# A hybrid decoder layer: the output projection begins with the first halves of four column tiles, and token sums of squares take fewer fp32 products

## The chip, the cores and the metric

The kernel runs on one core of a Trainium2 chip. The metric is the device time of one execution in microseconds (us). Before the change three runs gave 1185.44, 1186.08 and 1186.83 us; the median is 1186.08 us.

Engines are named as in the profile: PE is TensorE (products), PEld its weight load, DVE is VectorE, ACT is ScalarE, POOL is GpSimd, SP is SyncE, whose queue starts most DMAs. A queue executes its instructions in the order of the program, each when its waits are met.

## The reference

The reference computes one layer of a decoder in float32 for 256 tokens with 2048 channels (`x` below is one token's row):

```
h = rmsnorm(x, g_mix);  proj = h @ w_in            # 2048 x 5200
x = x + concat(pool_mixer(..), dsa_attention(..)) @ w_out      # 2048 x 2048
u = rmsnorm(x, g_ffn) @ w_up                       # 2048 x 11264
x = x + (silu(gate(conv3(u))) * val(conv3(u))) @ w_down        # 5632 x 2048
x = x + (p @ w_ple_proj) * sigmoid(rmsnorm(x, g_ple) @ w_ple_gate)
out = rmsnorm(x, g_final)
# rmsnorm(x, g) = x * (mean(x*x over channels) + 1e-6) ** -0.5 * g
```

The norm of a token is one number, r = (mean of squares + 1e-6)^-0.5. It multiplies a whole row, so the kernel multiplies the products by it afterwards and not their inputs.

## The kernel before, in words

**Layout.** Activations are kept with channels in the 128 partitions and tokens along the free axis: `xt` is [128, 16, 256], 16 tiles of 128 channels by 256 tokens. `hT` holds the layer's input times the gain, split in a rounded part (256 columns) and the rest (256 columns), so that float32 accuracy is had from products of the chip's fp32r kind.

**Units and column tiles.** A weight matrix is read in units of 128 x 1024 floats (`unit`, L74 to L89). The SP queue loads a unit into one of four `raw` buffers, ACT writes the rounded copy `hi` (L87), DVE writes the rest, `lo` = raw - hi (L88), a subtraction that reads two operands in SBUF. `hi` and `lo` of a unit lie in one of three buffers `w`, which the units take in turn, so unit k can be cast only when PE is done with unit k-3. A column tile (128 output channels) of a product with 2048 inputs needs two units, its halves. Each half is eight pairs of products on PE (`cm_matmul`, L143 to L149): `hi` against 512 columns (L147), `lo` against 256 (L148). The sum is built in one of four PSUM buffers of pool `acc` (name `pa`), taken in turn: tile k+4 waits until tile k has been read out.

**Stages.** In order: products with `w_in` and the mixers, the output projection with `w_out` (16 column tiles, L518 to L526), the up stage with `w_up` (88 tiles, two by two: a gate tile and a value tile), the down stage with `w_down` (16 tiles), the per-layer embedding with `w_pg` and the final norm.

**Output projection.** Its 16 input tiles are `catP` (pooling) and `catA` (attention), listed in `cats`. `out_unit(c, ps, h)` does half h of column tile c. Two tiles are taken at a time: both first halves, then both second halves. Among the first halves the last pooling group is mapped (`pool_map`, L470 to L488, its products are L483); the two `catP` tiles that come from it are the last of the second halves. `add_residual` (L179 to L186) adds a tile to `xt`, splits it into `hT` for the next stage and squares each pair of tiles into `ssa`, which holds the running sums of squares, [128, 512]: even tiles' tokens in columns 0 to 255, odd tiles' in 256 to 511.

**Sums of squares of tokens.** `rstd_tok` (L197 to L204) sums `ssa` over its partitions by products with ones: four fp32 products of 128 x 2, one for each half of `ssa` and each 128 tokens, which leave one number for each token in a column, [128, 2]. `rstd_col` and `rstd_of` (L119 to L134) make r from it: DVE scales and adds epsilon (L122), POOL raises to the power -0.5 (L128), DVE does one Newton step (L130, L131, L133). It is called for the mixer's norm (r_mix), the up stage's (r_ffn) and the embedding's (r_ple). Where r is needed along the free axis, `rstd_rows` (L136 to L141) multiplies it by the identity on PE and copies it into `rbc`, [128, 256] (L139, L141).

**Up stage.** `conv` (L542 to L554) takes a finished tile: `cm_evict` (L161 to L165) copies its right half (ACT, L163) into one of three buffers `eb`, adds the left half (DVE, L164), after which the PSUM buffer is free, and multiplies by `rbc` (DVE, L165), after which the `eb` buffer is free. A convolution of three taps over the tokens follows (ACT L549, DVE L551 and L553), then the gate (ACT L558, DVE L559) and a split (L112, L113).

**Order of the work.** The program lists instructions in the order of the functions; a list scheduler then moves them, engine by engine, by its own estimate of when each can start. The order on each engine is fixed before the kernel runs.

Of the kernel before, what the change touches and what calls it, by code (L numbers as in the profile page):

```python
# [10 lines left out]
F32 = mybir.dt.float32  # L11
F32R = mybir.dt.float32r
AF = mybir.ActivationFunctionType
OP = mybir.AluOpType
# [4 lines left out]
P = 128  # L19
S = 256  # L20
D = 2048
KT = D // P
# [4 lines left out]
EPS = 1e-6  # L27
# [10 lines left out]
AT_PG = (112, 1264)  # L38

GAP_G = 88  # L40
GAP_W, GAP_A, GAP_F = 144, 8, 176


C_GMIX, C_GFFN, C_GPLE, C_PS, C_CONV = 0, 16, 32, 48, 56
# [6 lines left out]
def layer(ctx: ExitStack, tc: tile.TileContext, a: dict):  # L51
    nc = tc.nc
    in_order = tc.keep_in_program_order
    V, A, T, G = nc.vector, nc.scalar, nc.tensor, nc.gpsimd
# [9 lines left out]
    rbc = mid[0].tile([P, S], F32, name="rbc")  # L64
    ssa = mid[0].tile([P, 2 * S], F32, name="ssa")
    wraw = ctx.enter_context(tc.tile_pool(name="wraw", bufs=4))
    tmp = ctx.enter_context(tc.tile_pool(name="tmp", bufs=2))
    dram = ctx.enter_context(tc.tile_pool(name="dram", bufs=1, space=DRAM))
    acc = ctx.enter_context(tc.tile_pool(name="acc", bufs=4, space=PSUM))
    aux = ctx.enter_context(tc.tile_pool(name="aux", bufs=4, space=PSUM))  # L70
# [3 lines left out]
    def unit(src, n=1024, keep=None, at=(0, LOW)):  # L74

        nonlocal n_units
        raw = wraw.tile([P, UNIT], F32, name="raw")
        nc.sync.dma_start(raw[:, :n], src)
        if keep:
            hi = keep.tile([P, n], F32R, name="hi", bufs=5)  # L80
            lo = keep.tile([P, n], F32R, name="lo", bufs=5)
        else:
            w = wsp[n_units % 3].tile([P, SLOT], F32R, name="w")
            n_units += 1
            h0, l0 = at if n <= 1024 else (0, UNIT)
            hi, lo = w[:, h0:h0 + n], w[:, l0:l0 + n]
        A.copy(hi, raw[:, :n])  # L87
        V.tensor_sub(lo, raw[:, :n], hi.bitcast(F32))  # L88
        return hi, lo  # L89
# [8 lines left out]
    mhalf = cst.tile([P, 2], F32, name="mhalf")  # L98
    G.memset(mhalf, -0.5)
    ones2 = cst.tile([P, 2], F32, name="ones2")  # L100
# [9 lines left out]
    def split(dst_hi, dst_lo, src, scale=None):  # L110
        if scale is None:
            A.copy(dst_hi, src)  # L112
            V.tensor_sub(dst_lo, src, dst_hi.bitcast(F32))  # L113
        else:
            A.activation(dst_hi, src, AF.Copy, scale=scale)
            V.scalar_tensor_tensor(dst_lo, src, scale, dst_hi.bitcast(F32),
                                   op0=OP.mult, op1=OP.subtract)

    def rstd_col(ssq, name):  # L119
        n = ssq.shape[1]  # L120
        ms = tmp.tile([P, n], F32, name="ms")
        V.tensor_scalar(ms, ssq, 1.0 / D, EPS, op0=OP.mult, op1=OP.add)  # L122
        return rstd_of(ms, name)

    def rstd_of(ms, name):
        n = ms.shape[1]
        r0 = tmp.tile([P, n], F32, name="r0")
        G.tensor_tensor(r0, ms, mhalf[:, :n], op=OP.pow)  # L128
        r1 = tmp.tile([P, n], F32, name="r1")
        V.tensor_mul(r1, r0, r0)  # L130
        V.scalar_tensor_tensor(r1, r1, -0.5, ms, op0=OP.mult, op1=OP.mult)  # L131
        r = cst.tile([P, n], F32, name=name)
        V.scalar_tensor_tensor(r, r1, 1.5, r0, op0=OP.add, op1=OP.mult)  # L133
        return r  # L134

    def rstd_rows(r):  # L136
        ps = aux.tile([P, 512], F32, name="ps")
        for t in range(2):
            T.matmul(ps[:, t * P:(t + 1) * P], r[:, t:t + 1].to_broadcast([P, P]), ident,  # L139
                     start=True, stop=True)  # L140
        V.tensor_copy(rbc, ps[:, :S])  # L141

    def cm_matmul(ps, hi, lo, acts, first, last):  # L143

        for i, act in enumerate(acts):
            w = slice(i * P, (i + 1) * P)
            T.matmul(ps, hi[:, w], act, start=first and i == 0, stop=False)  # L147
            T.matmul(ps[:, :S], lo[:, w], act[:, :S],  # L148
                     start=False, stop=last and i == len(acts) - 1)  # L149

    def tiles(act, kts):
        return [act[:, kt, :] for kt in kts]

    def cm_tile(src, c):
        ps = acc.tile([P, 512], F32, name="pa")
        for h in range(2):
            hi, lo = unit(src[c][:, h * 1024:(h + 1) * 1024])
            cm_matmul(ps, hi, lo, tiles(hT, range(8 * h, 8 * h + 8)), h == 0, h == 1)
        return ps

    def cm_evict(dst, ps):  # L161
        b = mid[1].tile([P, S], F32, name="eb", bufs=3)
        A.copy(b, ps[:, S:])  # L163
        V.tensor_add(b, ps[:, :S], b)  # L164
        V.tensor_mul(dst, b, rbc)  # L165
# [13 lines left out]
    def add_residual(c, ps, gcol):  # L179

        xs = xt[:, c, :]
        V.tensor_add(xs, ps[:, :S], xs)
        V.tensor_add(xs, ps[:, S:], xs)
        split(hT[:, c, :S], hT[:, c, S:], xs, prm[:, gcol + c:gcol + c + 1])
        if c % 2:
            square(c // 2)  # L186

    def square(i):
        pair = xt[:, 2 * i:2 * i + 2, :].rearrange("p k s -> p (k s)")
        if i == 0:  # L190
            A.activation(ssa, pair, AF.Square)
        else:
            sq = tmp.tile([P, 2 * S], F32, name="sq", bufs=1)
            A.activation(sq, pair, AF.Square)
            V.tensor_add(ssa, ssa, sq)

    def rstd_tok(name):  # L197

        ps = aux.tile([P, 512], F32, name="ps")
        for t in range(2):  # L200
            for h in range(2):
                T.matmul(ps[:, 2 * t:2 * t + 2], ssa[:, h * S + t * P:h * S + (t + 1) * P], ones2,
                         start=h == 0, stop=h == 1)
        return rstd_col(ps[:, 0:4:2], name)  # L204


    with ExitStack() as c1:
# [117 lines left out]
        for j in range(IH // 2):  # L325
            ps = cm_tile(a["w_qi"], j) if j else ps_q
# [187 lines left out]
        def out_unit(c, ps, h):  # L514
            hi, lo = unit(a["w_out"][c][:, h * 1024:(h + 1) * 1024])
            cm_matmul(ps, hi, lo, cats[8 * h:8 * h + 8], h == 0, h == 1)

        for c0 in range(0, KT, 2):  # L518
            ps2 = [acc.tile([P, 512], F32, name="pa") for _ in range(2)]
            for h in range(2):  # L520
                for e in range(2):
                    out_unit(c0 + e, ps2[e], h)
                    if c0 + h + e == 0:
                        pool_map(*done.pop())
            for e in range(2):
                add_residual(c0 + e, ps2[e], C_GFFN)  # L526


    pin = ctx.enter_context(tc.tile_pool(name="pin", bufs=1))
# [4 lines left out]
    with ExitStack() as c2:  # L534
        far = c2.enter_context(tc.tile_pool(name="far", bufs=1))
        far.tile([P, GAP_F], F32, name="gap_f")
        aT = far.tile([P, NF, 2 * S], F32R, name="aT")
        r_ffn = rstd_tok("r_ffn")
        rstd_rows(r_ffn)
        nu = 0  # L540

        def conv(ps, c):  # L542
            nonlocal nu
            u = ub[:, nu % NU, :]
            nu += 1
            cm_evict(u[:, 2:], ps)
            k = 4 * c
            t = far.tile([P, S], F32, name="cv", bufs=4)
            A.activation(t, u[:, 2:], AF.Identity, bias=cnv[:, k + 3:k + 4],  # L549
                         scale=cnv[:, k + 2:k + 3])  # L550
            V.scalar_tensor_tensor(t, u[:, 1:S + 1], cnv[:, k + 1:k + 2], t,  # L551
                                   op0=OP.mult, op1=OP.add)
            V.scalar_tensor_tensor(t, u[:, :S], cnv[:, k:k + 1], t, op0=OP.mult, op1=OP.add)  # L553
            return t  # L554

        def up_pair(c, ps2):
            ts = [conv(ps2[e], 2 * c + e) for e in range(2)]
            A.activation(ts[0], ts[0], AF.Silu)  # L558
            V.tensor_mul(ts[0], ts[0], ts[1])  # L559
            split(aT[:, c, :S], aT[:, c, S:], ts[0])  # L560

        ps2 = [acc.tile([P, 512], F32, name="pa") for _ in range(2)]
        for h in range(2):
            for e in range(2):
                hi, lo = unit(a["w_up"][e][:, h * 1024:(h + 1) * 1024])
                cm_matmul(ps2[e], hi, lo, tiles(hT, range(8 * h, 8 * h + 8)), h == 0, h == 1)
        up_pair(0, ps2)
        for c in range(1, NF):  # L570
            up_pair(c, [cm_tile(a["w_up"], 2 * c + e) for e in range(2)])


        for c in range(KT):
            ps = acc.tile([P, 512], F32, name="pa")
            for k0 in range(0, NF, 8):
                k1 = min(k0 + 8, NF)
                hi, lo = unit(a["w_down"][c][:, k0 * P:k1 * P], (k1 - k0) * P)
                cm_matmul(ps, hi, lo, tiles(aT, range(k0, k1)), k0 == 0, k1 == NF)
            add_residual(c, ps, C_GPLE)  # L580
# [175 lines left out]
```

## Time and profile before

| | |
|---|---|
| median of three runs | 1186.08 us |
| the profiled execution | 1187.71 us |
| its span, first to last instruction | 1185.9 us |
| PE busy | 1172.4 us, 99% |
| DVE busy | 854.6 us, 72% |
| ACT busy | 643.7 us, 54% |
| POOL busy | 9.0 us, 1% |
| chain that ended last | PE 98% |
| output projection begins, up stage begins | 260.2 us, 352.6 us |
| last product of the down stage begins | 1072.2 us |

The profile's busy time of PE is modelled, and its matmuls are pipelined; what a product costs is better read from the starts of the products around it. A row of the timeline gives start, duration, engine, line, operation, output <- inputs and shapes; several like instructions are merged into one row ("x8"), whose duration runs from the first start to the last end. An fp32 product leaves two records. A group row ends with busy time and mean duration in ns, and after the bar the idle time before the instructions with what ended it.

### The profile page before, as it was taken

The numbers are of one execution on the slowest core, as the hardware profiler recorded it, in microseconds if no ns is written. First come the engines' busy times: TensorE is split into PE (matmuls) and PEld (weight loads), VectorE is DVE, ScalarE is ACT, GpSimd is POOL, SyncE is SP. The second block draws the span as 40 slices with busy tenths as digits, with TensorE's granted clock in tenths as the row PEclk, the third lists the DMA queues.
The fourth block names the chain that finished last, engine by engine and source line by source line (L and its number), as shares of the span: only waits on it lengthen the run. The fifth ranks groups of instructions, "written<-read, shape, count | busy, mean of one in ns | idle before, by whom it ended". The sixth has DMA issues, their size and how long they took to land.

```text
span 1185.9 us, 17860 instructions
## 1 busy us (share of the span) xinstructions
PE 1172.4 (99%) x6804; PEld 1037.6 (87%) x6804; DVE 854.6 (72%) x1308; ACT 643.7 (54%) x943; POOL 9.0 (1%) x27
## 2 busy tenths in 40 slices
PE   9999999999999999999999999999999999999996
PEld 8988888888888888888888888888888888888886
DVE  6578977976678888888888888888555555554564
ACT  7466444554546666666666666666444444444563
POOL 0000000000000000000000000000000000000000
PEclk9999999999999999999999999999999999999998
DMA  8656765545565556556555556556666666666662
GB/s 310 212 175 190 236 215 173 162 147 189 189 194 185 195 194 195 195 192 194 192 194 193 195 192 195 192 196 194 186 194 194 195 194 191 191 193 226 191 214 75
DMA packets 66933, 229.09 MB, mean 193 GB/s; under 512 B 7872, under 2 KB 9672, under 8 KB 66720
## 3 DMA queue, kind: packets, MB, share of 16 engines
q1 hardware_dynamic: 63696, 221.91, 58.5%
q10 hardware_dynamic: 2144, 3.41, 0.9%
q0 software_dynamic: 1008, 2.64, 0.7%
q8 instruction: 53, 0.87, 0.3%
q14 instruction: 32, 0.26, 0.1%
HBM read 224.77 MB, written 3.68 MB: 193 GB/s over the span
## 4 chain that ended last, share of the span: by engine, by line
PE 98%; DMA 0%; ACT 0%; DVE 0%; SPq 0%; issue 0%; POOLq 0%; ACTq 0%
PE pa L147 55%; PE pa L148 28%; PE pa L175 3%; PE pa L176 3%; PE pa L174 3%; PE ps L176 1%; PE ps L175 1%; PE ps L174 1%; DMA raw<-in_w_first 0%; PE ps L483 0%; PE ps L393 0%; PE ps L147 0%; PE ps L310 0%; PE ps L311 0%; PE ps L607 0%; PE ps L444 0%
## 5 line engine op out<-in xcount | busy, mean ns | idle before, releaser
L88 DVE TENSOR_TENSOR w<-raw,w 128x1024 fp32r<-128x1024 f32 (+3 forms) x420 | 503.2, 1199 | 220.8 <-ACT w L87 214.0
L147 PE MATMUL pa<-hT,w 128*128 128x512 f32 x1904 | 652.5, 391 | 0.0
L87 ACT CAST w<-raw 128x1024 fp32r<-128x1024 f32 (+3 forms) x420 | 433.0, 1031 | 341.6 <-PE pa L148 250.6
L148 PE MATMUL pa<-hT,w 128*128 128x256 f32 x1904 | 529.6, 278 | 0.0
L147 PEld LDWEIGHTS pa<-hT,w 128*128 128x128 f32 x1904 | 357.5, 188 | 75.0 <-issue 0.6
L148 PEld LDWEIGHTS pa<-hT,w 128*128 128x128 f32 x1904 | 358.5, 188 | 0.3
L147 PE MATMUL pa<-aT,w 128*128 128x512 f32 x704 | 239.4, 390 | 0.0
L148 PE MATMUL pa<-aT,w 128*128 128x256 f32 x704 | 194.6, 276 | 0.0
L147 PEld LDWEIGHTS pa<-aT,w 128*128 128x128 f32 x704 | 132.2, 188 | 27.5
L148 PEld LDWEIGHTS pa<-aT,w 128*128 128x128 f32 x704 | 132.3, 188 | 0.0
L163 ACT COPY eb<-pa 128x256 f32<-128x256 f32 x119 | 44.2, 372 | 138.7 <-PE pa L148 138.5
L164 DVE TENSOR_TENSOR eb<-pa,eb 128x256 f32<-128x256 f32 x119 | 50.3, 423 | 59.8 <-ACT eb L163 59.6
L175 PE MATMUL pa<-w,hT 128*128 128x512 f32 (+2 forms) x178 | 64.8, 364 | 0.1
L176 PE MATMUL pa<-w,hT 128*128 128x512 f32 (+2 forms) x178 | 64.5, 363 | 0.0
L174 PE MATMUL pa<-w,hT 128*128 128x512 f32 (+2 forms) x178 | 58.0, 365 | 1.3 <-ACT w L87 1.3
L549 ACT ACTIVATE cv<-ub,cnv 128x256 f32<-128x256 f32 x88 | 52.9, 602 | 0.5 <-DVE ub L165 0.2
L147 PE MATMUL pa<-catA,w 128*128 128x512 f32 x128 | 46.9, 396 | 0.8 <-ACT w L87 0.8
L147 PE MATMUL pa<-catP,w 128*128 128x512 f32 x128 | 47.0, 396 | 0.0
L553 DVE SCALAR_TENSOR_TENSOR cv<-ub,cnv,cv 128x256 f32<-128x256 f32 x88 | 42.6, 485 | 3.0
L551 DVE SCALAR_TENSOR_TENSOR cv<-ub,cnv,cv 128x256 f32<-128x256 f32 x88 | 42.0, 479 | 0.1
L165 DVE TENSOR_TENSOR ub<-eb,rbc 128x256 f32<-128x256 f32 x88 | 37.3, 425 | 3.0
L174 PEld LDWEIGHTS pa<-w,hT 128*128 128x128 f32 x178 | 32.8, 188 | 5.8 <-ACT w L87 2.0
(171 smaller groups left out, 848.1 us busy)
## 6 DMA issues: line engine op xcount, KB each, us to landing
raw<-in_w_up SPq DMA_DIRECT2D x176, 512.0 KB, 4.6
raw<-in_w_down SPq DMA_DIRECT2D x80, 512.0 KB, 3.9
raw<-in_w_qk SPq DMA_DIRECT2D x32, 512.0 KB, 4.2
raw<-in_w_out SPq DMA_DIRECT2D x32, 512.0 KB, 4.5
raw<-in_w_pg SPq DMA_DIRECT2D x32, 512.0 KB, 4.0
raw<-in_w_first SPq DMA_DIRECT2D x15, 552.0 KB, 5.8
raw<-in_w_qi SPq DMA_DIRECT2D x16, 512.0 KB, 4.0
raw<-in_w_u SPq DMA_DIRECT2D x16, 512.0 KB, 3.9
```

What stands on the lines that cost most here:

```text
L87: A.copy(hi, raw[:, :n])
L88: V.tensor_sub(lo, raw[:, :n], hi.bitcast(F32))
L147: T.matmul(ps, hi[:, w], act, start=first and i == 0, stop=False)
L148: T.matmul(ps[:, :S], lo[:, w], act[:, :S], start=False, stop=last and i == len(acts) - 1)
L163: A.copy(b, ps[:, S:])
L164: V.tensor_add(b, ps[:, :S], b)
L174: T.matmul(pss[t][:, :n], xh, hi[:, w], start=first and i == 0, stop=False)
L175: T.matmul(pss[t][:, :n], xh, lo[:, w], start=False, stop=False)
L176: T.matmul(pss[t][:, :n], xl, hi[:, w], start=False, stop=last and i == len(kts) - 1)
L549: A.activation(t, u[:, 2:], AF.Identity, bias=cnv[:, k + 3:k + 4], scale=cnv[:, k + 2:k + 3])
L551: V.scalar_tensor_tensor(t, u[:, 1:S + 1], cnv[:, k + 1:k + 2], t, op0=OP.mult, op1=OP.add)
L553: V.scalar_tensor_tensor(t, u[:, :S], cnv[:, k:k + 1], t, op0=OP.mult, op1=OP.add)
```

## The change

There are three edits.

1. In the output projection the first four column tiles are taken together: four first halves, then four second halves. The other twelve tiles go two by two as before. The number of products, units and bytes is the same.
2. `rstd_tok` first adds the two halves of `ssa` on DVE (128 x 256) and then needs two products instead of four. It remains in use for r_mix and r_ple.
3. For the up stage a new function, `rstd_all`, replaces `rstd_tok` and `rstd_rows`. One fp32 product of a matrix of ones with `ssa` (256 columns) puts every token's sum into every partition, so r is computed at once as a row in all partitions: the scaling (L213 of the new file), the power on POOL (L214), the Newton step (L215 to L217), each on 128 x 256 instead of 128 x 2. Its result is `rbc` itself. The scratch tile is `sq` of pool `tmp`.

A spacer, `GAP_W`, grows by 8 columns (32 bytes a partition), while the small tile `r_ffn` is gone.

```
-GAP_W, GAP_A, GAP_F = 144, 8, 176
+GAP_W, GAP_A, GAP_F = 152, 8, 176
...
     def rstd_tok(name):
 
         ps = aux.tile([P, 512], F32, name="ps")
+        V.tensor_add(ssa[:, :S], ssa[:, :S], ssa[:, S:])
         for t in range(2):
-            for h in range(2):
-                T.matmul(ps[:, 2 * t:2 * t + 2], ssa[:, h * S + t * P:h * S + (t + 1) * P], ones2,
-                         start=h == 0, stop=h == 1)
+            T.matmul(ps[:, 2 * t:2 * t + 2], ssa[:, t * P:(t + 1) * P], ones2,
+                     start=True, stop=True)
         return rstd_col(ps[:, 0:4:2], name)
+
+    def rstd_all():
+
+        ps = aux.tile([P, 512], F32, name="ps")
+        V.tensor_add(ssa[:, :S], ssa[:, :S], ssa[:, S:])
+        T.matmul(ps[:, :S], ones2[:, :1].to_broadcast([P, P]), ssa[:, :S], start=True, stop=True)
+        two = tmp.tile([P, 2 * S], F32, name="sq", bufs=1)
+        ms, r0 = two[:, :S], two[:, S:]
+        V.tensor_scalar(ms, ps[:, :S], 1.0 / D, EPS, op0=OP.mult, op1=OP.add)
+        G.tensor_tensor(r0, ms, mhalf[:, :1].to_broadcast([P, S]), op=OP.pow)
+        V.tensor_mul(rbc, r0, r0)
+        V.scalar_tensor_tensor(rbc, rbc, -0.5, ms, op0=OP.mult, op1=OP.mult)
+        V.scalar_tensor_tensor(rbc, rbc, 1.5, r0, op0=OP.add, op1=OP.mult)
...
-        for c0 in range(0, KT, 2):
-            ps2 = [acc.tile([P, 512], F32, name="pa") for _ in range(2)]
+        for c0, cn in ((0, 4), *((c, 2) for c in range(4, KT, 2))):
+            pss = [acc.tile([P, 512], F32, name="pa") for _ in range(cn)]
             for h in range(2):
-                for e in range(2):
-                    out_unit(c0 + e, ps2[e], h)
+                for e in range(cn):
+                    out_unit(c0 + e, pss[e], h)
                     if c0 + h + e == 0:
                         pool_map(*done.pop())
-            for e in range(2):
-                add_residual(c0 + e, ps2[e], C_GFFN)
+            for e in range(cn):
+                add_residual(c0 + e, pss[e], C_GFFN)
...
-        r_ffn = rstd_tok("r_ffn")
-        rstd_rows(r_ffn)
+        rstd_all()
```

Three places show how instructions are moved. A name with a number is one buffer or one use of it: `w_3939` is a unit's hi/lo pair, `pa_3661` a tile's sum, `eb_3712` its copy. Lines from 200 on are those of the new file in the rows of the changed kernel.

The first place is DVE at the beginning of the up stage. Before, the chain of r_ffn (L122 to L133), the copy into `rbc` (L141) and the first multiplication by it (L165) stand among the first subtractions:

```order
L122 TENSOR_SCALAR ms_3509<-ps_3504 128x2
L130 TENSOR_TENSOR r1_3513<-r0_3511 128x2
L164 TENSOR_TENSOR eb_3608<-pa_3522,eb_3608 128x256
L131 SCALAR_TENSOR_TENSOR r1_3513<-r1_3513,ms_3509 128x2
L133 SCALAR_TENSOR_TENSOR r_ffn_3516<-r1_3513,r0_3511 128x2
L88 TENSOR_TENSOR w_3652<-raw_3650,w_3652 128x1024
L164 TENSOR_TENSOR eb_3616<-pa_3523,eb_3616 128x256
L88 TENSOR_TENSOR w_3674<-raw_3672,w_3674 128x1024
L141 COPY rbc_77<-ps_3518 128x256
L165 TENSOR_TENSOR ub_106<-eb_3608,rbc_77 128x256
```

Now, on the same engine at the same place (`w_3664` is the first unit of the fourth tile, `w_3939` the first of the ninth, tiles counted from 1):

```order
L88 TENSOR_TENSOR w_3642<-raw_3640,w_3642 128x1024
L213 TENSOR_SCALAR sq_3506<-ps_3503 128x256
L164 TENSOR_TENSOR eb_3606<-pa_3513,eb_3606 128x256
L88 TENSOR_TENSOR w_3664<-raw_3662,w_3664 128x1024
...
L88 TENSOR_TENSOR w_3939<-raw_3937,w_3939 128x1024
L215 TENSOR_TENSOR rbc_77<-sq_3506 128x256
L216 SCALAR_TENSOR_TENSOR rbc_77<-rbc_77,sq_3506 128x256
L217 SCALAR_TENSOR_TENSOR rbc_77<-rbc_77,sq_3506 128x256
L165 TENSOR_TENSOR ub_106<-eb_3598,rbc_77 128x256
L165 TENSOR_TENSOR ub_106<-eb_3606,rbc_77 128x256
L165 TENSOR_TENSOR ub_106<-eb_3704,rbc_77 128x256
```

Between the scaling (L213) and the Newton step (L215) stand eleven subtractions L88, from `w_3664` to `w_3939`, and the multiplications L165 of the first three tiles are behind them. The power on POOL lies between L213 and L215.

The second place is ACT a little later, in the changed kernel. `cv_3602` is the first tile's convolution, and `eb_3712` the copy of the fourth tile, whose PSUM buffer the eighth tile takes:

```order
L87 CAST w_3876<-raw_3874 128x1024
L87 CAST w_3897<-raw_3895 128x1024
L87 CAST w_3939<-raw_3937 128x1024
L562 ACTIVATE cv_3602<-ub_106,cnv_96 128x256
L163 COPY eb_3712<-pa_3661 128x256
```

The copy of the fourth tile stands behind the cast of the ninth tile's first unit and behind the first tile's convolution; before, each tile's copy stood among the casts of the next tile.

The third place is PE in the output projection, at the step from the third unit of `w_out` to what follows. Before, both second halves (`w_2762`, `w_2783`) belong to the two tiles just begun (`pa_2692`, `pa_2693`), and their last products use the two late `catP` tiles; a third tile (`pa_2811`) begins between them. One row is given for each step to another unit:

```order
L147 MATMUL pa_2692<-catA_2080,w_2762 128x512
...
L147 MATMUL pa_2811<-catP_117,w_2815 128x512
...
L147 MATMUL pa_2693<-catA_2080,w_2783 128x512
L147 MATMUL pa_2692<-catP_117,w_2762 128x512
...
L147 MATMUL pa_2812<-catP_117,w_2836 128x512
L147 MATMUL pa_2811<-catA_2080,w_2857 128x512
```

Now the first halves of the third and fourth tile (`w_2763`, `w_2784`) come in between:

```order
L147 MATMUL pa_2693<-catP_117,w_2763 128x512
...
L147 MATMUL pa_2691<-catA_2079,w_2805 128x512
...
L147 MATMUL pa_2694<-catP_117,w_2784 128x512
L147 MATMUL pa_2691<-catP_117,w_2805 128x512
...
L147 MATMUL pa_2692<-catA_2079,w_2826 128x512
```

Behind the third and fourth tile's first halves the second halves of tiles one and two (`w_2805`, `w_2826`) follow, and no new tile begins among them.

## Rows read from the trace of the kernel before

**Rows 1.** The page: busy time by engine; the chain that ended last.
```profile
PE 1172.4 (99%) x6804; PEld 1037.6 (87%) x6804; DVE 854.6 (72%) x1308; ACT 643.7 (54%) x943; POOL 9.0 (1%) x27
...
PE 98%; DMA 0%; ACT 0%; DVE 0%; SPq 0%; issue 0%; POOLq 0%; ACTq 0%
```

**Rows 2.** Timeline of PE: start us, us, engine, line, names, shapes; sums for r_ffn.
```profile
360.55 0.95 PE L202 MATMUL ps<-ones,ssa 128*128 128x2 f32 x8
...
361.56 0.40 PE L147 MATMUL pa<-hT,w 128*128 128x512 f32 x1
```

**Rows 3.** Timeline of PE: one fp32 product of 256 columns among pairs.
```profile
181.50 0.59 PE L393 MATMUL ps<-qk 128*128 128x256 f32 x2
...
182.04 0.40 PE L147 MATMUL pa<-hT,w 128*128 128x512 f32 x1
```

**Rows 4.** Timeline of PE: r_ffn turned into rows.
```profile
366.56 0.61 PE L139 MATMUL ps<-ident,r_ffn 128*128 128x128 f32 x4
...
367.13 0.40 PE L147 MATMUL pa<-hT,w 128*128 128x512 f32 x1
```

**Rows 5.** Timeline of PE in the output projection, from 275.5 us.
```profile
275.51 0.28 PE L148 MATMUL pa<-catP,w 128*128 128x256 f32 x1
...
277.10 0.50 PE L147 MATMUL pa<-catA,w 128*128 128x512 f32 x1 [0.84 <-ACT w L87]
...
277.66 0.39 PE L147 MATMUL pa<-catP,w 128*128 128x512 f32 x1
...
278.01 0.39 PE L147 MATMUL pa<-catP,w 128*128 128x512 f32 x1
```

**Rows 6.** Timeline of POOL: four of the five powers.
```profile
59.33 1.77 POOL L128 TENSOR_TENSOR r<-ms,mhalf 128x2 f32<-128x2 f32 x1 [57.92 <-DVE ms L122]
...
361.78 0.73 POOL L128 TENSOR_TENSOR r<-ms,mhalf 128x2 f32<-128x2 f32 x1 [128.46 <-DVE ms L122]
1083.39 0.69 POOL L128 TENSOR_TENSOR r<-ms,mhalf 128x2 f32<-128x2 f32 x1 [720.88 <-DVE ms L122]
1168.04 0.55 POOL L128 TENSOR_TENSOR r<-ms,mhalf 128x1 f32<-128x1 f32 x1 [83.96 <-DVE ms L624]
```

**Rows 7.** Timeline of DVE: a subtraction at 59.31, and one at 363.47.
```profile
59.31 1.23 DVE L88 TENSOR_TENSOR w<-raw,w 128x1024 fp32r<-128x1024 f32 x1
...
363.47 1.23 DVE L88 TENSOR_TENSOR w<-raw,w 128x1024 fp32r<-128x1024 f32 x1 [0.17 <-ACT w L87]
```

**Rows 8.** Timeline of PE: tiles four and eight of the up stage begin.
```profile
370.56 0.39 PE L147 MATMUL pa<-hT,w 128*128 128x512 f32 x1
...
392.32 0.39 PE L147 MATMUL pa<-hT,w 128*128 128x512 f32 x1
```

**Rows 9.** Groups of DVE and ACT, 390 to 867 us, by form.
```profile
L88 DVE TENSOR_TENSOR w<-raw,w 128x1024 fp32r<-128x1024 f32 x175 | 214.1, 1224 | 32.2 <-ACT w L87 26.9
...
L551 DVE SCALAR_TENSOR_TENSOR cv<-ub,cnv,cv 128x256 f32<-128x256 f32 x83 | 39.7, 479 | 0.0
L165 DVE TENSOR_TENSOR ub<-eb,rbc 128x256 f32<-128x256 f32 x82 | 34.9, 425 | 2.8
...
L87 ACT CAST w<-raw 128x1024 fp32r<-128x1024 f32 x175 | 184.1, 1052 | 83.7 <-PE pa L148 82.4 <-issue 1.3
L549 ACT ACTIVATE cv<-ub,cnv 128x256 f32<-128x256 f32 x82 | 49.4, 602 | 0.2
L163 ACT COPY eb<-pa 128x256 f32<-128x256 f32 x82 | 30.5, 372 | 96.5 <-PE pa L148 96.5
```

**Rows 10.** Engines by stretch: length, busy PE, PEld, DVE, ACT, POOL; clock, DMA.
```profile
390.60:867.00 476.40, 476.40 (x2805) 421.70 (x2804) 386.42 (x594) 286.40 (x426) 0.00 (x0) 1.00 0.60 193
...
1176.00:1178.40 2.40, 0.00 (x0) 0.00 (x0) 1.49 (x4) 0.91 (x3) 0.09 (x1) 1.00 0.00 0
1178.40:1185.90 7.50, 0.00 (x0) 0.00 (x0) 1.36 (x5) 1.33 (x2) 0.46 (x1) 0.50 0.42 140
```

**Rows 11.** Timeline of PE: its first products.
```profile
1.17 3.48 PE L226 MATMUL ps<-rbc 128*128 128x256 f32 x8 [1.17 <-POOL rbc L104]
```

## The prediction

> **What bounds the kernel.** I read the page first. PE is busy for 99% of the span and makes up 98% of the chain that ended last [rows 1], so a microsecond that PE works less or waits less is a microsecond of the result, and so is one that it waits more. Next comes PE's timeline, for the products that the change removes and for PE's waits. The reader should go by the starts there: one pair of L147 and L148 takes 0.35 us in the output projection (277.66 to 278.01) [rows 5] and 0.34 us in the up stage (64 pairs from 370.56 to 392.32) [rows 8]. Last come POOL's powers [rows 6] and what DVE did beside them [rows 7], because the change puts a power of 256 columns where one of 2 was. POOL is busy 1% of the time [rows 1], but that says nothing of an instruction that does not occur yet.
>
> **The gains.** A stretch of the timeline costs its length less the L148 that lies in it, a third of a pair (its share of the columns), 0.12 us. Eight records of L202 took 361.56 - 360.55 - 0.12 = 0.89 us [rows 2]. For r_mix and r_ple half of them go: 2 x 0.445 = 0.89 us. For the up stage all eight go, and the four records of L139, 367.13 - 366.56 - 0.12 = 0.45 us [rows 4]; a product of 256 columns comes, which by its like costs 182.04 - 181.50 - 0.12 = 0.42 us [rows 3]. That is 0.92 us, all before the fourth tile of the up stage.
>
> In the output projection PE lost time from 275.51 to 277.66: 2.15 us for two pairs, so 1.45 us of waiting, on a cast (L87) [rows 5]. The unit that it waited for needed the buffer of a second half, whose last products use the late `catP` tiles. In the new order two more first halves lie ahead of these, 5.6 us of PE's work. I take the whole 1.45 us as gained; the other end is nothing, or a new wait of that size.
>
> Gains together: 0.89 + 0.92 + 1.45 = 3.3 us. The added DVE sums (three of 128 x 256, 0.43 us each by L165 [rows 9]) stand before subtractions that DVE does well ahead of the product which reads them; were that cover gone, they cost 0.43 us each. The spacer and the vanished small tile cost nothing by themselves; should addresses matter to PE, the price is that of the pace rival below.
>
> **The power.** One column took 0.55 us, two columns 0.69 and 0.73 us where nothing lay beside them [rows 6], so the second column cost 0.14 to 0.18 us. No row shows more than two. If each column costs that, 256 columns take 0.55 + 255 x 0.14 = 36.3 us, or 46.5 us by 0.18. The other end is that columns beyond the first are nearly free, about 1 us. I take 36.3 us, since only these rows show the operation, and the smaller step was the later one.
>
> It starts after the scaling L213, which DVE does behind the sixth unit's subtraction. That one ended at 363.47 + 1.23 = 364.70 [rows 7] and comes 0.89 us earlier, at 363.8; with 0.42 for L213 the power starts at about 364.3 and ends at 400.6.
>
> **The first wait: DVE held.** The power at 59.33 took 1.77 us in place of 0.69 or 0.73 [rows 6]. It is the only one with a subtraction L88 beside it, from 59.31 to 60.54 [rows 7], and it ended 0.56 us after that, which is a power's own time. So the power did not run beside an instruction that reads two operands in SBUF. I choose to read this as exclusion both ways: whoever starts first holds the other off to its end. The price of the other reading, a first call that is slow for its own sake, is the first rival.
>
> [...]
>
> Then the subtraction of `w_3664`, the fourth tile's first unit, waits until 400.6, and everything behind it in DVE's queue with it. It takes 1.22 us [rows 9], to 401.85 with the hand-over. PE has the first three tiles' units by then and begins the fourth at 370.56 - 0.92 = 369.64 [rows 8]; its first product needs only `hi`, its second needs `lo`, at 369.87. PE waits 32.0 us (no exclusion: 0; a step of 0.18: 42.2).
>
> **The second wait: the order behind the power.** L215 to L217 stand in DVE's queue behind the subtraction of `w_3939`. That unit's cast needs the buffer of the seventh tile's second unit, so it begins when PE is done with the seventh tile, and by then all four PSUM buffers are full: `rbc` does not exist, three tiles sit in `eb`, and the eighth tile needs the fourth's buffer. From the end of the seventh tile to the first product of the eighth there follow, by [rows 9], the cast 1.05, the subtraction 1.22, L215 0.43, L216 and L217 0.48 each, the first L165 0.43, the first tile's convolution on ACT (it stands ahead of the copy) 0.60, the copy 0.37 and L164 0.42: 5.5 us, and 0.2 for hand-overs, 5.7 us. This comes whatever the power costs.
>
> **What follows from the waits.** DVE has 476.4 - 386.4 = 90 us to spare in 476.4 [rows 10], 19%. At the second restart it owes the convolutions of seven tiles, and about 19 instructions of some 0.43 us and one subtraction stand ahead of the first `lo` that PE lacks: 9.4 us, where three finished units give PE 8.2 us of work. So 1.2 us are lost there and something at the next units; I take 2.0 us, between 0 and 5.
>
> [...] The first eight records of the program took 3.48 us, 0.43 each [rows 11], against 0.21 for the same form later [rows 3]: a cold start loses about 1.6 us before the rate doubles. I take it to fall in both waits: 3.2 us, between 0 and 3.4.
>
> **The sum.** -3.3 + 32.0 + 5.7 + 2.0 + 3.2 = +39.6 us. The profiled execution took 1187.71 us, 1.8 us of it outside its span of 1185.9, and would take 1227.3 us. It was 1.6 us above the median of the runs, 1186.08 us, against which the result will be read: 1225.7 us. With the bounds of the parts, mostly the step of 0.18, this case reaches from 1219 to 1240 us.
>
> **Rivals.**
> No exclusion, but a long power. DVE goes on with its subtractions, and L215 waits for 400.6 instead of for `w_3939`. Then 0.43 + 0.48 + 0.48 + 0.43 + 0.60 + 0.37 + 0.42 + 0.2 = 3.4 us bring PE to 404.0, where the eighth tile would have begun at 392.32 - 0.92 = 391.4: 12.6 us, with 2.0 and one cold start 1.6, less 3.3: +12.9 us, 1199.0 us. For it: the trace shows only POOL held up, and the 1.77 us belong to the first call. Against: the end 0.56 us behind the subtraction's end. Chance 18%.
>
> A short power. The step from one to two columns is then a start-up step, and the power ends after about a microsecond. The first wait vanishes, the second stays: -3.3 + 5.7 + 2.0 + 1.6 = +6.0 us, 1192.1 us. Against it: two powers of two columns agree within 0.04 us, and both are longer than the one of one column. Chance 15%. [...]
>
> A slower pace afterwards. PE ran at 0.35 us a pair before r_ffn's products and at 0.34 behind them [rows 5, 8]. If PE comes out of the waits at 0.35, the 81 tiles from the eighth on (16 pairs each) and the down stage (16 tiles of 44 pairs) make 2000 pairs: +20 us on the forecast, 1245.7 us. For it: the pace has no cause in the program that I can see. Against: nothing but that it held for 700 us. Chance 18%.
>
> Faster. The power is short and PE does not wait at the eighth tile, so that only the gains remain: 1182.8 us. The place is the copy of the fourth tile; it decides when the chain of 5.7 us from the seventh tile's end falls under 3.3 us. Against it stands that each link is there in the order of DVE or ACT and has a measured length. Chance 4%.
>
> **How the numbers follow.** The forecast has 40%, and 5% are left for a power that costs still more per column than 0.18 us. The range 1197 to 1250 us takes in the forecast, the slower pace and the long power without exclusion; the short power and the faster case, 19%, are mostly left out. A difference under 0.2%, 2.4 us, can't be told from none. Faster has 3%, no difference 3% (the rest of the last rival and the best of the short power), slower 94%.
>
> **What would show it.** The power L214 in POOL's rows: 36 us (right), about 1 us (the short power). A subtraction L88 that begins only when it ends, and PE waiting for DVE in the fourth tile for 32 us, show the exclusion; subtractions that go on beside it show the first rival. PE waiting some 6 us before the eighth tile shows the second wait. In the output projection no product should wait for a cast. A pair's length behind 440 us tells the pace. The forecast is wrong if POOL's row is short or DVE is not held.

## The result and the profile after

The changed kernel is slower: 1.0115 times the kernel before (95% interval 1.0102 to 1.0129) in the first comparison, and 1.0132 (1.0116 to 1.0147) in a second one with more runs, 1201.18 us against 1185.47. That is +13.6 to +15.7 us, where the forecast had +39.6. The sign held and the size did not; the time lies at the first rival's 1199.0 us. Three of the first six runs, and some later ones of kernels with this wait, took 1220 to 1228 us at the same granted clock of 0.99 and stand outside the comparisons; why they differ is open. The rows of this section are from an execution of 1200.92 us.

The page of the profile after, with busy time by engine and the chain that ended last, answers to [rows 1]:

```profile
PE 1171.0 (98%) x6786; PEld 1037.3 (87%) x6786; DVE 855.2 (71%) x1310; ACT 643.8 (54%) x943; POOL 48.4 (4%) x27
...
PE 95%; POOL 3%; DVE 1%; ACT 0%; DMA 0%; issue 0%; SPq 0%; POOLq 0%; ACTq 0%
```

POOL's busy time grew from 9.0 to 48.4 us, and POOL now has 3% of the chain that sets the end. PE's busy time fell by 1.4 us while the span grew by 13.2, so what grew is the time in which PE does nothing. The list of PE's waits (tile and line that waited, on whom: total us, times, longest) has three rows:

```profile
PE pa L147 <- DVE eb L164: 16.5, 1, 16.5
PE ps L239 <- POOL rbc L104: 1.2, 1, 1.2
PE pa L174 <- ACT w L87: 0.4, 1, 0.4
```

The second of these was there before [rows 11]. The first is the loss, and POOL's timeline has its source. It answers to [rows 6]:

```profile
57.99 0.70 POOL L128 TENSOR_TENSOR r<-ms,mhalf 128x2 f32<-128x2 f32 x1 [56.59 <-DVE ms L122]
358.98 41.17 POOL L214 TENSOR_TENSOR sq<-sq,mhalf 128x256 f32<-128x256 f32 x1 [127.22 <-DVE sq L213]
```

The power lasts 41.17 us, to 400.15. The groups of DVE from 358.9 to 400.2 us, by form, show what ran beside it (busy us, mean ns, then the idle time before them and who ended it); compare [rows 7]:

```profile
L88 DVE TENSOR_TENSOR w<-raw,w 128x1024 fp32r<-128x1024 f32 x11 | 13.5, 1225 | 14.7 <-ACT w L87 14.7
L164 DVE TENSOR_TENSOR eb<-pa,eb 128x256 f32<-128x256 f32 x2 | 0.8, 425 | 1.6 <-ACT eb L163 1.6
L215 DVE TENSOR_TENSOR rbc<-sq 128x256 f32<-128x256 f32 x1 | 0.4, 426 | 10.8 <-POOL sq L214 10.8
```

Eleven subtractions ran inside the power, each in 1225 ns, which is what they take with POOL idle [rows 9]. DVE was not held. Its idle time beside the power was spent on casts (14.7 us) and copies (1.6 us), and at the end it stood 10.8 us for the power's result. The last of the eleven, that of `w_3939`, and L215 behind it:

```profile
388.19 1.23 DVE L88 TENSOR_TENSOR w<-raw,w 128x1024 fp32r<-128x1024 f32 x1 [1.57 <-ACT w L87]
400.19 0.43 DVE L215 TENSOR_TENSOR rbc<-sq 128x256 f32<-128x256 f32 x1 [10.77 <-POOL sq L214]
```

PE's timeline at the eighth tile answers to the second row of [rows 8]:

```profile
386.80 0.28 PE L148 MATMUL pa<-hT,w 128*128 128x256 f32 x1
403.62 0.77 PE L147 MATMUL pa<-hT,w 128*128 128x512 f32 x1 [16.55 <-DVE eb L164]
...
404.40 0.63 PE L147 MATMUL pa<-hT,w 128*128 128x512 f32 x1
...
405.04 0.63 PE L147 MATMUL pa<-hT,w 128*128 128x512 f32 x1
...
408.24 0.45 PE L147 MATMUL pa<-hT,w 128*128 128x512 f32 x1
...
408.64 0.39 PE L147 MATMUL pa<-hT,w 128*128 128x512 f32 x1
```

The first seven tiles are multiplied by 387.1; the eighth has no PSUM buffer until the fourth is copied out, and that copy needs a free `eb`, which needs `rbc`. The first product starts 403.62 - 400.15 = 3.5 us behind the power's end. Then seven pairs take 0.64 us each. The windows (length, busy PE, PEld, DVE, ACT, POOL, granted clock, DMA share, GB/s) say why:

```profile
387.00:391.00 4.00, 0.07 (x1) 0.00 (x0) 1.23 (x1) 1.04 (x1) 4.00 (x1) 1.00 0.52 175
391.60:403.60 12.00, 0.00 (x0) 0.01 (x1) 3.31 (x9) 1.58 (x5) 8.55 (x1) 0.50 0.06 20
403.60:408.20 4.60, 4.58 (x14) 3.93 (x15) 4.34 (x13) 3.66 (x8) 0.00 (x0) 0.50 0.00 0
408.20:412.00 3.80, 3.80 (x24) 3.36 (x23) 3.76 (x9) 3.77 (x9) 0.00 (x0) 0.98 0.00 0
```

PE had no products from 387.1; the granted clock was 1.00 up to 391.0 and 0.50 from 391.6, and rose 4.6 us after the restart. In that time 403.62 to 408.24 hold seven pairs that take 7 x 0.34 = 2.4 us elsewhere: 2.2 us lost. Behind 408.6 PE has no further wait in the up stage.

In the output projection the wait of [rows 5] is gone: the list of PE's waits above has no L147 that waited for a cast. Around the same place a pair takes its 0.35 us (274.97 to 275.32):

```profile
274.97 0.39 PE L147 MATMUL pa<-catP,w 128*128 128x512 f32 x1
275.20 0.28 PE L148 MATMUL pa<-catP,w 128*128 128x256 f32 x1
275.32 0.40 PE L147 MATMUL pa<-catA,w 128*128 128x512 f32 x1
```

### The profile page after: what moved, and what is told of

Same layout as the page of the kernel before. It is cut to its first block, busy times and chain, and to the rows that moved or that the text cites. A ratio compares the mean times of both kernels' runs of the same rounds, so it can differ in the third digit from the quotient of the medians.

```text
span 1226.3 us, 17826 instructions
## 1 busy us (share of the span) xinstructions
PE 1197.8 (98%) x6786; PEld 1049.6 (86%) x6786; DVE 858.4 (70%) x1310; ACT 643.2 (52%) x943; POOL 48.4 (4%) x27
## 4 chain that ended last, share of the span: by engine, by line
PE 94%; POOL 3%; DVE 1%; DMA 0%; ACT 0%; SPq 0%; issue 0%; POOLq 0%; ACTq 0%
PE pa L147 53%; PE pa L148 27%; POOL sq L214 3%; PE pa L175 3%; PE pa L176 3%; PE pa L174 3%; PE ps L175 1%; PE ps L176 1%; PE ps L174 1%; DMA raw<-in_w_first 0%; PE ps L496 0%; PE ps L406 0%; PE ps L147 0%; PE ps L323 0%; PE ps L324 0%; PE ps L620 0%
## 5 line engine op out<-in xcount | busy, mean ns | idle before, releaser
L147 PE MATMUL pa<-hT,w 128*128 128x512 f32 x1904 | 672.3, 396 | 16.5 <-DVE eb L164 16.5
L88 DVE TENSOR_TENSOR w<-raw,w 128x1024 fp32r<-128x1024 f32 (+3 forms) x420 | 503.4, 1199 | 242.2 <-ACT w L87 236.1
L148 PE MATMUL pa<-hT,w 128*128 128x256 f32 x1904 | 536.0, 282 | 0.0
L147 PEld LDWEIGHTS pa<-hT,w 128*128 128x128 f32 x1904 | 358.0, 188 | 101.4 <-issue 17.5
L148 PEld LDWEIGHTS pa<-hT,w 128*128 128x128 f32 x1904 | 359.1, 189 | 0.4
L147 PE MATMUL pa<-aT,w 128*128 128x512 f32 x704 | 248.8, 396 | 0.0
L148 PE MATMUL pa<-aT,w 128*128 128x256 f32 x704 | 197.7, 281 | 0.0
L147 PEld LDWEIGHTS pa<-aT,w 128*128 128x128 f32 x704 | 132.0, 188 | 32.4
L148 PEld LDWEIGHTS pa<-aT,w 128*128 128x128 f32 x704 | 132.2, 188 | 0.0
L164 DVE TENSOR_TENSOR eb<-pa,eb 128x256 f32<-128x256 f32 x119 | 50.3, 423 | 68.7 <-ACT eb L163 68.5
L214 POOL TENSOR_TENSOR sq<-sq,mhalf 128x256 f32<-128x256 f32 x1 | 41.2, 41172 | 127.2 <-DVE sq L213 127.2
L147 PE MATMUL pa<-catP,w 128*128 128x512 f32 x128 | 45.9, 391 | 0.0
L147 PE MATMUL pa<-catA,w 128*128 128x512 f32 x128 | 45.6, 390 | 0.0
L165 DVE TENSOR_TENSOR ub<-eb,rbc 128x256 f32<-128x256 f32 x88 | 37.2, 424 | 2.8
```

The lines of the kernel that those rows point to most:

```text
L148: T.matmul(ps[:, :S], lo[:, w], act[:, :S], start=False, stop=last and i == len(acts) - 1)
L214: G.tensor_tensor(r0, ms, mhalf[:, :1].to_broadcast([P, S]), op=OP.pow)
```

## The experiments

Two theories stood at the start. A: the power's length is the price, through the order of the eighth tile, as in the first rival; DVE is not held. B: the power costs something by itself, or the rest of the change is slow too. Each kernel ran beside the kernel before on the same chip.

**The change again, nothing edited** (a_again).

> The changed kernel once more, for a trace of it whose pairs run at 0.34 us. Long power without exclusion (the first rival, now the leading theory): about 1200.6 us, POOL's power about 41 us, subtractions on DVE of 1.23 us beside it, one wait of PE of about 17 us before the eighth tile of the up stage and none in the fourth. Exclusion (the forecast's mechanism): a wait of some 32 us in the fourth tile. Pace theory (the pairs' length is the cost and the wait is not): where pairs take 0.34 us throughout, the time is that of the kernel before.

Measured: 1201.18 us, ratio 1.0132 (1.0116 to 1.0147). The rows above are from it: one wait of 16.5 us before the eighth tile and none in the fourth, although the pairs behind the wait take 0.340 us.

**All but the rows** (b_columns): the new projection order and the sums by fewer products stay, the up stage gets its r by columns.

```
-GAP_W, GAP_A, GAP_F = 152, 8, 176
+GAP_W, GAP_A, GAP_F = 144, 8, 176
...
-        rstd_all()
+        r_ffn = rstd_tok("r_ffn")
+        rstd_rows(r_ffn)
```

> The change with r_ffn made by columns as before (two products, power of 2 columns, turned into rows); first halves of four tiles and two products for each sum stay. Long power: nothing of the cost is left, and the gains show: 0.45 us for each of three sums and 1.45 us in the output projection, 2.8 us, and up to 2.6 us more if the output projection keeps the faster pace of pairs: 1181 to 1184 us, ratio 0.996 to 0.998. If the output projection's new order were the cause (its end leaves PE or the buffers in a worse state): 1198 to 1201 us.

Measured: 1181.67 us, ratio 0.9968 (0.9956 to 0.9979). It beats both kernels. So everything that the change loses is in the rows. Its trace also tells whether DVE holds POOL up; the rows of DVE and of POOL:

```profile
357.51 1.23 DVE L88 TENSOR_TENSOR w<-raw,w 128x1024 fp32r<-128x1024 f32 x1
```

```profile
357.68 1.65 POOL L128 TENSOR_TENSOR r<-ms,mhalf 128x2 f32<-128x2 f32 x1 [125.91 <-DVE ms L122]
```

A power of two columns that comes 0.17 us behind a subtraction ends 0.59 us after that ends; at 59.33 in the kernel before it was 0.56 us [rows 6, 7]. It is not the first power of this kernel: that one, at 57.98 with no subtraction running, took 0.70 us. So the 1.77 us of the kernel before were a hold-up of POOL by DVE, and not a slow first call. The other traces agree: every power of two columns that began while an L88 ran took 1.65 to 1.77 us (five powers in five kernels), every other 0.69 to 0.73 us, also where an L88 began while the power ran.

**The rows alone** (c_rows_only): the kernel before with `rstd_all` for the up stage; projection and the other sums as before. The function itself is added as in the change.

```
-GAP_W, GAP_A, GAP_F = 144, 8, 176
+GAP_W, GAP_A, GAP_F = 152, 8, 176
...
-        r_ffn = rstd_tok("r_ffn")
-        rstd_rows(r_ffn)
+        rstd_all()
```

> The kernel before with r_ffn alone made as rows at once; output projection in pairs and four products for the other sums as before. Long power: the whole wait of 16 to 17 us and 1.7 us of cold clock, less 0.9 us of products: 1186 + 17 = 1203 us, ratio about 1.014. If the output projection's order were the cause: 1185 us.

Measured: 1229.26 us, ratio 1.0366 (1.0336 to 1.0397): missed by some 26 us. The power takes 41.17 us again and PE waits 16.5 us at the eighth tile again, so the miss lies elsewhere. The count of L147 in 200 us of the up stage shows it (stretch, length, busy PE with the count, clock, DMA share, GB/s); first this kernel, then the changed one:

```profile
440.00:640.00 200.00, 200.00 (x568) 1.00 0.57 187
```

```profile
440.00:640.00 200.00, 200.00 (x589) 1.00 0.59 194
```

With no wait in that stretch and the clock at 1.00 in both, a pair takes 200 / 568 = 0.352 us instead of 200 / 589 = 0.340. Over the 2000 pairs behind the wait this is 25 us. The pace of the prediction's third rival exists, and something sets it. With the old order of the projection the pairs took 0.35 us ahead of the product too (115 L147 from 300 to 340 us).

**No power** (d_no_power): the changed kernel, with a multiplication in the power's place; the up-stage norm is left out.

```
-        G.tensor_tensor(r0, ms, mhalf[:, :1].to_broadcast([P, S]), op=OP.pow)
+        G.tensor_tensor(r0, ms, mhalf[:, :1].to_broadcast([P, S]), op=OP.mult)
```

> The changed kernel with a multiplication on POOL in place of the power (the up stage's norm is then left out and the output is another). All else of the rows is there: the product of 256 columns, the scaling, the Newton step on 128 x 256. Long power: no wait is left, 1181 to 1184 us. If the rows cost by their product, their 128 x 256 instructions on DVE or their place in the order: still 6 us or more above the kernel before, 1192 us.

Measured: 1201.97 us, ratio 1.0139 (1.0124 to 1.0155): missed by 18 us or more, and by chance near the changed kernel's time. POOL's instruction takes 0.62 us, PE has no wait in the up stage and the mean granted clock is 0.997, as in the kernel before, so all that theory A prices is gone. What came instead is the pace:

```profile
440.00:640.00 200.00, 200.00 (x572) 1.00 0.57 188
```

It is 0.350 us behind the 256-column product (356.80), and 0.347 from 800 to 860 us (173 L147); before that product it was 0.340. In the changed kernel too the pairs take 0.35 us from the product on, until PE stops; behind the stop, with the clock back at 1.00, they take 0.340.

The edit changes the order as well: the scheduler has put L215 ahead of the next subtraction, where the changed kernel has eleven between. So the wait's end is not due to the shorter instruction alone.

```profile
359.92 0.41 DVE L215 TENSOR_TENSOR rbc<-sq 128x256 f32<-128x256 f32 x1
```

**Half the power** (h_half): the power on 128 columns, a multiplication on the rest.

```
-        G.tensor_tensor(r0, ms, mhalf[:, :1].to_broadcast([P, S]), op=OP.pow)
+        G.tensor_tensor(r0[:, :P], ms[:, :P], mhalf[:, :1].to_broadcast([P, P]), op=OP.pow)
+        G.tensor_tensor(r0[:, P:], ms[:, P:], mhalf[:, :1].to_broadcast([P, P]), op=OP.mult)
```

> The changed kernel with the power on the first 128 of the 256 columns only; the other 128 are multiplied in a second GpSimd instruction, so the up-stage norm of half of the tokens is left out. Theory A (the power's length by columns is the whole of the first wait): GpSimd holds its power for 0.55 + 127 x 0.16 = about 20.8 us instead of 41.2, that is it ends some 21 us earlier, 4 us before TensorE comes to the eighth tile: no wait of TensorE above 0.1 us there, VectorE not idle before the square, the clock at 1.00 throughout. Since nothing then stops TensorE, the pair pace that follows the 256-column product stays to the end: with 0.350 us for a pair, as in the kernel without a power, 1202 us; with 0.340, 1182. Theory B (a fixed cost of a power on a wide tile, not by columns): the power still takes over 35 us, TensorE waits over 10 us, 1195 us or more with a wait in the trace.

Measured: 1202.73 us, ratio 1.0138 (1.0124 to 1.0152). POOL's rows, and PE's wait at the eighth tile:

```profile
358.47 20.77 POOL L214 TENSOR_TENSOR sq<-sq,mhalf 128x128 f32<-128x128 f32 x1 [127.36 <-DVE sq L213]
379.23 0.39 POOL L215 TENSOR_TENSOR sq<-sq,mhalf 128x128 f32<-128x128 f32 x1
```

```profile
PE pa L147 <- DVE eb L164: 0.7, 1, 0.7
```

The power goes by columns, 0.16 us each, and the wait shrinks from 16.5 to 0.7 us, not quite to nothing: between the first multiplications by `rbc` and L164 of the fourth tile a subtraction and a convolution step stand in DVE's queue. The order has moved here too: the square, L216 in this file, stands behind eight subtractions and not eleven, so the shorter power and the earlier place act together.

```profile
380.63 0.41 DVE L216 TENSOR_TENSOR rbc<-sq 128x256 f32<-128x256 f32 x1
```

Without a stop the slow pace stays (573 L147 from 440 to 640 us, 173 from 800 to 860). Theory B, a fixed cost of a wide power, is excluded by the 20.77 us, and the pace is a second, separate price.

**The product in two halves** (j_two_halves), without the power, so that nothing else disturbs the pace; the up-stage norm is left out.

```
-        T.matmul(ps[:, :S], ones2[:, :1].to_broadcast([P, P]), ssa[:, :S], start=True, stop=True)
+        for t in range(2):
+            T.matmul(ps[:, t * P:(t + 1) * P], ones2[:, :1].to_broadcast([P, P]),
+                     ssa[:, t * P:(t + 1) * P], start=True, stop=True)
```

> The kernel without the power (GpSimd multiplies; the up-stage norm is left out), and the sum of squares over the tokens by two fp32 products of 128 columns in place of one of 256. Theory A (which of the two pair paces TensorE holds, 0.340 or 0.350 us, is set by what stands between two runs of pairs, here the product, and stays until the next such place): another composition may set the other pace; with 0.340 from the product to the end 1182 us, with 0.350 1202; a pace that changes anywhere between the product and the next interlude speaks against it. Theory B (the slow pace comes from what the rows path does on VectorE and GpSimd or from where its tiles lie, not from the product): 0.350 and 1202 us whatever the product's form.

Measured: 1181.47 us, ratio 0.9959 (0.9947 to 0.9972), 21.3 us less than the next kernel, which ran beside it. The pace behind the product:

```profile
440.00:640.00 200.00, 200.00 (x589) 1.00 0.60 194
```

In d_no_power the product stands at the same place, behind 27 pairs of the up stage, the tiles are the same, and the instructions of the rows path stand in the same order on DVE and POOL; there the pace was the slow one, here it is the fast one. So theory B falls: it is the form of the product, and not the rows path, that makes this difference.

**One product more** (k_extra_product), without the power; the up-stage norm is left out.

```
         T.matmul(ps[:, :S], ones2[:, :1].to_broadcast([P, P]), ssa[:, :S], start=True, stop=True)
+        T.matmul(ps[:, S:S + 2], ssa[:, :P], ones2, start=True, stop=True)
```

> The kernel without the power (the up-stage norm is left out), with one more fp32 product of two columns behind the 256-column one, whose result nobody reads. It costs about 0.11 us by itself. Theory A (the pair pace is set at the interlude): TensorE may come out of it at 0.340 us a pair, and the time is then 1182 us, 20 us less for one instruction more; else 1202. Theory B (the rows path sets the slow pace): 1202 us.

Measured: 1202.76 us, ratio 1.0138 (1.0124 to 1.0152): the slow pace stays (573 L147 in the same 200 us). By itself this run fits both theories. PE has as many products here as in j_two_halves (the changed kernel's 6786 records and two more in both), so their number does not decide the pace; which compositions help was not settled.

**Two-product sums alone** (f_two_products): the new `rstd_tok` at all three places, in the kernel before. It needs two products where there were four, which left eight records.

> The kernel before with only the new way of summing the squares over the tokens (two fp32 products and one addition on VectorE in place of eight products), at all three places; output projection and up stage as before. Theory A (the sum of the forecast): three times 0.445 us, 1.3 us less than the kernel before, 1184.2 us. Theory B (the interludes also set the pair pace): a shift by the stretches whose pace changes, between 5 us less and 20 us more, and where the pace changes is seen at the product's place.

Measured: 1184.09 us against 1186.55, ratio 0.9983 (0.9974 to 0.9992). The forecast's 1.3 us are inside the interval, and the pace is that of the kernel before: 115, 590 and 178 L147 in 300 to 340, 440 to 640 and 800 to 860 us, where that has 115, 589 and 178.

**The projection's order alone** (e_out_only), in the kernel before.

```
-        for c0 in range(0, KT, 2):
-            ps2 = [acc.tile([P, 512], F32, name="pa") for _ in range(2)]
+        for c0, cn in ((0, 4), *((c, 2) for c in range(4, KT, 2))):
+            pss = [acc.tile([P, 512], F32, name="pa") for _ in range(cn)]
...
```

> The kernel before with only the new beginning of the output projection (first halves of four column tiles, then their second halves); sums of squares and up stage as before. Theory A (the sum of the forecast): the wait of 1.11 us at the ninth product of the projection goes, and the clock stays as it was: 1.1 to 1.5 us less than the kernel before of the same call, ratio 0.9987 to 0.9990; with the up stage by columns and fewer sums it and the kernel with the two-product sums alone (0.9983 measured) should add up to the kernel with both (0.9968). Theory B (moving the interludes also moves the pair pace): where the pace from 280 us to the up stage goes from 0.350 to 0.340, as in the changed kernel, another 80 us / 0.35 x 0.01 = 2.3 us less, 3.4 to 3.8 us in all, ratio 0.9968 to 0.9971.

Measured: 1183.45 us against 1186.71, ratio 0.9974 (0.9964 to 0.9984). The wait's 1.1 to 1.5 us alone (0.9987 to 0.9990) lie outside the interval; with the pace they fit. The ratios of this kernel and of f_two_products give 0.9957 together; b_columns, which has both edits, measured 0.9968 (0.9956 to 0.9979), so they add up within the intervals. From 300 to 340 us, the kernel before and this one:

```profile
300.00:340.00 40.00, 40.00 (x115) 1.00 0.58 188
```

```profile
300.00:340.00 40.00, 40.00 (x119) 1.00 0.62 196
```

**Power and two halves** (l_after_two_halves): the changed kernel with the split product of j_two_halves.

> The changed kernel, power and all, with its sum of squares by two fp32 products of 128 columns in place of one of 256. Theory A (the wait before the eighth tile and the slow pace are two separate prices): the power still lasts 41.2 us, TensorE still waits 16 to 18 us before the eighth tile and pays 1.7 us at the half clock, while the pairs between the product and the wait now run at 0.340 us. The sum: 1181.5 (the kernel without a power and with two halves) + 16.5 + 0.9 (28 to 30 us of pairs are 0.9 us shorter, and the wait longer by as much, so about 17.4) + 1.7 = about 1200.6. Behind the wait the pace is set anew, by nothing in the program that differs: at 0.340 us to the end, 1200 to 1201 us, at 0.350, 1225 to 1228; both occurred in the changed kernel. Theory B (the product's form alone decides the pace for the rest, across the wait too): every run at 1200 to 1201 us.

Measured: ratio 1.0121 (1.0103 to 1.0139), about 1201 us where the sum gave 1200.6. PE's wait:

```profile
PE pa L147 <- DVE eb L164: 17.4, 1, 17.4
```

The wait is 17.4 us, as the sum had it: PE comes 0.9 us earlier to the eighth tile and waits as much longer. In the profiled run the pairs behind the wait take 0.340 us (589 L147 from 440 to 640 us). Theory B, which asked for 1200 to 1201 us in every run, is not borne out; what decides the pace after such a stop is open.

## Why the prediction was wrong

**The step that failed** is the first wait, "I choose to read this as exclusion both ways". The runs show one direction only. A power of two columns waits for a subtraction that is already running (1.77 and 1.65 us in place of 0.70). A running power of 256 columns holds up none of eleven subtractions (1225 ns each). Nor do they hold up the running power: 0.16 us a column lies between 2 and 128 columns and between 128 and 256, with 13.5 us of subtractions beside the longest. Why the power waits only at its start is not shown. The 32.0 us in the fourth tile are therefore zero. The row that the choice rested on was read correctly and then turned round without a row. A GpSimd multiplication may differ from a power here: in h_half one subtraction that started 0.05 us behind the multiplication took 1.43 us instead of 1.23. One row does not show it.

**What took its place** is the first rival, a wait for the power's result, with its place and its links: 3.4 us forecast from the power's end to the eighth tile's product, 3.5 measured. Its 12.6 us became 16.5 because the power was longer, 41.2 us where the small step of [rows 6] gave 36.3; 0.16 us a column lies between the two steps. Of these 4.9 us 0.9 did not show, since PE came later to the eighth tile at the slow pace. That the rival's sum, 1199.0 us, comes so near is in part luck: its wait was 3.9 us too short, and 2.0 us of backlog in it did not occur.

**The second wait**, 5.7 us for the order of L215 behind the subtraction of `w_3939`, is no extra term: the subtraction ended at 389.42, the power at 400.15, and one wait covers both. By that order alone PE would have begun the eighth tile at about 389.42 + 3.5 = 392.9, an estimate from these rows, 5.8 us behind the seventh; the other 10.7 us of the wait are the power's. No run shows this order with a short power, since a shorter one also moved L215. **The backlog**, 2.0 us, measured nothing in the changed kernel. **The cold start** came once, not twice, and cost 2.2 us, where 1.6 were taken. The row that this was read from gives 3.48 - 8 x 0.21 = 1.8 us, and the profile has the granted clock at 1.00 there, so it was no row of the lower clock. No run shows the sum's 3.2 us for a clock that falls in both waits: the granted clock fell in the one wait of 16.5 us.

**The gains** were 3.3 us on paper. The 1.45 us in them should have been 1.33: the stretch of 2.15 us holds an L148 (0.12 us) besides its two pairs. The kernel with all of the gains but those of the up stage's single product is 3.8 us faster than before (2.5 to 5.2 by its interval). About 2.3 us were not foreseen: the new order of the projection also brings the fast pace from 280 us to the up stage (80 us, 3% shorter). With the 2.7 us that were foreseen for this kernel that is 5.0 us, at the upper end of the interval.

**The pace** was a rival at the wrong place: not the restart from the wait but the 256-column product sets it to 0.35 us, for 30 us, 85 pairs and 0.9 us, until PE stops. What pace PE comes back in after the stop is open.

The sum as the runs have it: -3.8 (b_columns), -0.5 (the product in place of the remaining sums and rows, by the forecast's 0.92 less 0.445), +0.9 pace, +16.5 wait, +2.2 clock: +15.3 us. Measured side by side: 1201.18 - 1185.47 = +15.7.

The range's lower end, 1197 us, reached to the first rival and held the time.

## What to carry to other kernels

A row that shows engine X waiting for engine Y is evidence for that direction alone; price the other direction as unknown. The power on GpSimd took 0.70 us for two columns, 20.77 for 128 and 41.17 for 256, so turn two columns into 256 only where 41 us of it fit before its reader. Where a scheduler sets the order, an edit of one instruction moves others, so read the order again before an experiment is put down to that instruction alone. Before a microsecond of products is saved on a full TensorE, count the pairs per 200 us after the edit: the pace that they came back in was worth 20.5 to 21.3 us here, where the up stage's sums and rows had 0.92 to save.

## What the runs showed of the hardware

- A power on GpSimd took 0.55 us for one column, 0.70 for two, 20.77 for 128 and 41.17 for 256; 256 columns of multiplication took 0.62 us.
- Pairs of a 512- and a 256-column product run at 0.340 or at 0.350 to 0.352 us with the granted clock at 1.00, for hundreds of microseconds. An fp32 product between them can change the pace: one of 256 columns set the slow one in the changed kernel and three others, two of 128 columns at the same place kept the fast one (1201.97 and 1202.76 against 1181.47 us without the power). Why is not settled.
- A power of two columns that began while DVE ran a subtraction of two operands in SBUF took 1.65 to 1.77 us, otherwise 0.69 to 0.73. Eleven such subtractions beside a running power of 256 columns took 1225 ns each, as with POOL idle.
- After 16.5 us without products PE worked 4.6 us at the clock of 0.50, and lost 2.2 us.
